# Two attention heads share a run of matmuls, rotary keys are padded to full height, and a planner's matmul durations are changed

## The chip, the core and the metric

The kernel runs on one NeuronCore of a Trainium2 chip. The metric is device time in microseconds (us) for one execution of the whole program; lower is better. The core's engines work side by side, each with its own queue in program order: TensorE (PE) multiplies matrices into PSUM, VectorE (DVE) and ScalarE (ACT) do elementwise work and reductions, GpSimd (POOL) small side work, and SyncE (SP) issues the transfers from DRAM. PE loads one operand of a matmul ahead of it; the profile shows these loads as a line of their own, PEld.

## What is computed

Four transformer layers over 256 tokens of width 1024, all in float32: a layer with block attention (MoBA) and forgetting attention (FOX), one with differential and sliding-window attention, and two blocks of latent or stick-breaking attention, cross attention to a memory and a squared-ReLU MLP. The change touches the attention of the first two layers and the latent attention (MLA) of the third. Cut to these:

```python
HEAD_DIM = 64                      # MoBA, FOX, differential maps, sliding window: 8 heads each (4 x 2 maps)
MLA_HEADS, MLA_NOPE, MLA_ROPE, MLA_V = 8, 128, 64, 128

def fox_attention(q, k, v, log_f):            # (B, H, S, 64); MoBA with one block is the same with another bias
    ...
        s = (jnp.einsum('bhqd,bhsd->bhqs', qb, k).astype(jnp.float32) * scale
             + cb[..., None] - c[:, :, None, :])
        s = jnp.where(tpos[:, None] >= kpos[None, :], s, -jnp.inf)
        p = jax.nn.softmax(s, axis=-1).astype(v.dtype)
        return jnp.einsum('bhqs,bhsd->bhqd', p, v)

def diff_attention(q, k, v, lam, slopes):     # two maps for each of 4 heads, 64 deep, values 128 wide
    ...
        p = jax.nn.softmax(s, axis=-1)
        a = (p[:, :, 0] - lam * p[:, :, 1]).astype(v.dtype)
        return jnp.einsum('bhqs,bhse->bhqe', a, v)

def swa_attention(q, k, v, sinks, slopes):    # 8 query heads, 2 key heads, window of 128
    ...

def mla_mixer(h, cos, sin, w_dkv, g_q, g_kv, w_uq, w_ukv, w_o):
    ...
    q_pe = apply_rope(q[..., MLA_NOPE:], cos, sin)
    k_pe = apply_rope(k_pe, cos, sin)
    q = jnp.concatenate([q[..., :MLA_NOPE], q_pe], axis=-1)
    k = jnp.concatenate([kv[..., :MLA_NOPE],
                         jnp.broadcast_to(k_pe, (B, S, MLA_HEADS, MLA_ROPE))], axis=-1)
    v = kv[..., MLA_NOPE:]
    o = blocked_causal_softmax_attn(q, k, v, (MLA_NOPE + MLA_ROPE) ** -0.5)
    return o.reshape(B, S, MLA_HEADS * MLA_V) @ w_o
```

## The kernel before

**Two passes.** `describe` first records every instruction of the network, with no address and no order between engines (`Plan.op`, `make`). Then `Plan.schedule` (L244) simulates the engines: it gives every instruction a duration from `make` (L472), keeps a queue for each engine by critical path and boost, lets an instruction start when what it depends on is done, and picks the engine for those that any of several may run (`either`). What comes out is a fixed order for each engine and a slot for each tile. All compute instructions are emitted from one line, L533, so the profile's rows have that line and are told apart by shape and tile. The tile names are those of the pools: `psum` the eight PSUM banks, `r` float32r tiles (the halves of split weights and activations), `k` float32 tiles; the order adds the tile's number (`psum_114`).

**Projections** are done as three float32r matmuls each (high by high, high by low, low by high half). A weight piece of 512 KB comes by DMA, ACT copies its high half, DVE subtracts the low half. These float32r matmuls are most of PE's 6829 instructions, and the planner puts them between the attention's steps.

**Attention** is in float32, where one product is two instructions on PE. Tokens are two tiles of 128, and the causal blocks are (first queries, first keys), 128 columns, and (second queries, all keys), 256 columns. The heads are 64 deep and two heads share a transposed tile: one on partitions 0 to 63, one on 64 to 127. For each head `scores` (L997) multiplies its 64 rows into a PSUM bank of its own, `soft` does the softmax on DVE and ACT, `probs_T` transposes the probabilities on PE, and `pv_feat` (L1078) multiplies values of 64 columns by them, into partitions 0 to 63 or 64 to 127 of one bank for the pair: a product with the first keys (256 columns) and one with the second (128). So a score matmul is 64 rows of the array by 128 columns (64\*128 in the profile), a value matmul 128 by 64 (128\*64), and everything else that matters 128 by 128. There are 16 pairs of score heads or maps (eight in the first layer, four differential, four sliding window) and 12 pairs of value products (eight and four; the differential values are 128 wide).

**Latent attention** (L1267) has eight heads with 128 plain dimensions and 64 rotary ones. The rotary queries of two heads share a tile by halves; the one rotary key, the same for all heads, is stored twice, in either half (`kpT`, L1319). The scores are a full-height product plus a 64-row one on the head's half, for each causal block.

The planner's durations for PE are the lines below; a float32r matmul of 256 columns counts as 109 ns.

```python
        elif mv.dtype == F32R:
            cost = N * (1 if N >= 256 else 4) / 2.4 + 2
        else:
            cost = 2 * max(2 * N / 2.4, load) + 2
```

Of the kernel before, what the change touches and what calls it, by code (L numbers as in the profile page):

```python
# [15 lines left out]
OP = mybir.AluOpType  # L16
# [4 lines left out]
# ======================================================================  # L21
# Recording: views of tiles that have no address yet
# ======================================================================
class Buf:
    """A tile to be: its slot is picked when its first instruction is scheduled."""

    def __init__(self, tag, np_, shape, dtype, name):
        self.tag, self.np_, self.dtype, self.name = tag, np_, dtype, name
        self.row = int(np.prod(shape))
        self.log = []          # (op, writes, p0, p1, mask)  # L30
        self.left = 0          # accesses not scheduled yet
        self.slot = None
        self.free_at = 0.0
        self.first = self.last = None


class Pool:
    """Slots for tiles. use[i]: the slots in use while instruction i runs, if from now on all
    instructions ran in the order of the program; as long as that fits, no deadlock is possible."""
# [114 lines left out]
# how long after the end of an instruction another engine may start  # L154
# [11 lines left out]
class Plan:  # L166
# [7 lines left out]
    # -- tiles  # L174
# [3 lines left out]
    def tag(self, name, pool, most=99, dtype=F32):  # L178
        """A kind of tile that lives in a pool, at most `most` at a time as long as others wait."""
# [12 lines left out]
    # -- instructions  # L192
    def op(self, forms, reads, writes, kind=""):
        """forms: {engine: (ns, call)}: the engines it may run on."""
        o = Op()
# [5 lines left out]
        for v, w in [(v, False) for v in reads] + [(v, True) for v in writes]:  # L201
# [13 lines left out]
            for e in b.log:  # L215
# [4 lines left out]
                # an older access that this write hides entirely need not be kept  # L220
# [11 lines left out]
    def either(self, *calls):  # L232
        """One instruction that any of several engines may run: (engine, method, args, kw) each."""
# [9 lines left out]
    # -- scheduling  # L243
    def schedule(self):  # L244
# [36 lines left out]
        def can(b):  # L281
            tg = self.tags[b.tag]
            p = tg["pool"]
            if b.first <= front:
                return bool(p.free)
            if not p.free or tg["used"] >= tg["most"]:
                return False
            return p.use[front:b.first].max() < p.bufs
# [11 lines left out]
        while n < len(ops):  # L300
# [23 lines left out]
            if e == "T":  # L324
                # the first by priority that the loading of its operand doesn't delay
# [10 lines left out]
            bad = next((b for b in news if not can(b)), None)  # L336
# [3 lines left out]
            # another engine that would be done with it sooner  # L340
# [71 lines left out]
    # -- emission  # L412
# [34 lines left out]
class _Eng:  # L447
    """Stands for an engine while the instructions are recorded."""
# [23 lines left out]
def make(plan, e, method, args, kw):  # L472
    """((cost, call), reads, writes, act tables) of one instruction."""
# [11 lines left out]
    if e == "T":  # L485
# [6 lines left out]
        elif mv.dtype == F32R:  # L492
            cost = N * (1 if N >= 256 else 4) / 2.4 + 2
        else:
            cost = 2 * max(2 * N / 2.4, load) + 2
# [57 lines left out]
# pools of tiles: elements in a partition, tiles  # L553
POOLS = {"k4": (1024, 5), "k2": (512, 33), "r2": (512, 46), "k1": (256, 18), "k128": (128, 11), "k16": (16, 64),
         "kr": (128, 3), "psum": (512, 8)}
# kinds of tiles: pool, the most at a time
# [8 lines left out]
class Net:  # L565
# [26 lines left out]
    def copy(self, out, in_):  # L592
        """A copy, on ACT or DVE."""
# [6 lines left out]
    def wpiece(self, src, f, pat, fill="", parts=1, **kw):  # L600
        """One piece of a weight matrix, f elements in each partition, as hi and lo in parts of equal size."""
# [15 lines left out]
    def wtiles(self, w, k0, nk, c0, nc_, fill=""):  # L617
        """Weight rows of the chunks k0.., columns c0..: pieces of (hi, lo, first chunk, chunks)."""
# [23 lines left out]
    def new_T(self, n=NC8):  # L642
        """(hi, lo) of a transposed activation: a list over the chunks of [128, 256] views each."""
# [9 lines left out]
    def mm3(self, ps, st, mv, first, last):  # L653
        """ps += st.T mv, both operands as (hi, lo)."""
# [5 lines left out]
    def mm_tok(self, ps, xt, wh, wl, kc, kmap, t, first, last):  # L660
        """ps[tokens of t, :] += X W, the activations stationary."""
# [8 lines left out]
    def proj_tok(self, w, xt, c0, ncol, k0=0, nk=NC8, ps=None, first=True, last=True, x0=0, cls="acc", fill=""):  # L670
        """Both token tiles of X W[:, c0:c0+ncol] in PSUM."""
# [7 lines left out]
    def mm_feat(self, ps, first_in_bank, xt, wh, wl, c, last):  # L679
        """ps[features, 256 tokens] += W.T X.T for a chunk, the weights stationary."""  # L680
# [5 lines left out]
    def proj_feat(self, w, xt, c0, ncol, nk=NC8, cls=("acc", "acc"), fill=""):  # L686
        """W[:, c0:c0+ncol].T X.T: feature blocks of 128, two to a bank."""
# [20 lines left out]
    def rows_T(self, tag, n, parts):  # L708
        """Rows of 128 from DRAM, transposed into columns [128, n]."""
# [88 lines left out]
    def squares(self, x):  # L798
        """Sums of the squares of the rows, [128, tiles]; x[t] has two halves."""
# [14 lines left out]
    def setup_late(self):  # L814
# [22 lines left out]
        nc.vector.tensor_scalar(self.lam, self.lam, LAM_INIT, None, op0=OP.subtract)  # -lambda  # L837
# [31 lines left out]
    def new_x(self):  # L869
        """The residual's transpose: banks of two chunks, [128, 2, 256] each."""  # L870
        return [self.nc.tile([128, 2, 256], "x", "x") for _ in range(4)]

    def stats_sum(self, x):
        """x: [128, k, 256] views; the sums of squares over the features, [128 tokens, tiles] in PSUM."""
# [18 lines left out]
    def stats_x(self, ss=None):  # L893
        """rstd of the residual's rows: [128, tiles]."""
# [11 lines left out]
    def gained(self, x, g0):  # L906
        """x.T times the gain, as hi and lo."""
# [11 lines left out]
    def rstd_bc(self, r):  # L919
        """rstd along the free dimension, the same in every partition: [128, 256]."""  # L920
# [10 lines left out]
    def out_proj(self, w, yt, pieces):  # L931
        """x += (Y W).T for a [*, 1024] matrix; pieces: (first chunk, chunks, half of the columns)."""
# [757 lines left out]
```

## Time and profile before

| | |
|---|---|
| three runs | 987.92, 986.16, 987.67 us; median 987.67 |
| profiled execution, span from its first to its last instruction | 990.0 us (its own time beside the span is not given) |
| PE busy | 962.9 us (97%), 6829 matmuls |
| DVE busy | 680.6 us (69%) |
| ACT busy | 571.4 us (58%) |
| POOL busy | 59.9 us (6%) |
| mean granted clock of PE | 0.994 of 2.4 GHz |

A row of the timeline gives the start of a group of like instructions that follow each other, the time from that start to the modelled end of the last, the engine, line and operation, the tiles written and read, the first one's shape (rows\*columns of the array, then the moving operand) and their number. Matmuls overlap, so the distance from one start to the next is the time that PE gives to one; the length of a row is longer than that by the part of the last one's end that lies beside the next. A row of the windows gives the busy time of each engine in a stretch, with the number of its instructions, then the granted clock and the DMA share.

### The profile page before, as it was taken

The page shows a single profiled execution, that of the slowest core. Times are in us where ns is not written, and L with a number is a line of the kernel's source. Part 1 is how long each engine was busy: PE and PEld are TensorE (multiplying, and loading weights), DVE is VectorE, ACT ScalarE, POOL GpSimd, SP SyncE. Part 2 cuts the span into 40 slices and gives each one's busy share as a digit, 9 for nine tenths or more (in the row PEclk, how much of TensorE's full clock was granted, in tenths as well). Part 3 has the DMA queues.
Part 4 walks back from the last instruction along what each step waited for, and adds up shares of the span by engine and source line. Part 5 has one row for each costly group of instructions (what it writes and reads, how often), then busy time and mean ns, then how long its engine had stood idle before and what let it go on. Part 6 is the DMA issues. An engine that isn't in the chain of part 4 may idle for free.

```text
span 990.0 us, 18191 instructions
## 1 busy us (share of the span) xinstructions
PE 962.9 (97%) x6829; PEld 874.0 (88%) x6829; DVE 680.6 (69%) x1561; ACT 571.4 (58%) x1310; POOL 59.9 (6%) x94
## 2 busy tenths in 40 slices
PE   7899999999999999999999999899999999999997
PEld 5577778888979889999999999899899999999985
DVE  7687686787987854896655456765768777556654
ACT  5675585557676675775555445644666754344443
POOL 2124000040210200000000000000000000000000
PEclk9999999999999999999999999999999999999999
DMA  7978424654413523664565456635535554555641
GB/s 193 285 191 207 113 85 150 212 149 131 145 34 90 154 94 115 211 192 141 171 204 180 149 192 203 181 128 165 166 117 168 174 170 144 179 189 176 203 154 43
DMA packets 96678, 157.13 MB, mean 159 GB/s; under 512 B 9831, under 2 KB 28493, under 8 KB 96589
## 3 DMA queue, kind: packets, MB, share of 16 engines
q1 hardware_dynamic: 96236, 154.91, 50.8%
q8 instruction: 53, 0.87, 0.4%
q0 software_dynamic: 352, 1.06, 0.3%
q14 instruction: 37, 0.30, 0.1%
HBM read 154.89 MB, written 1.06 MB: 158 GB/s over the span
## 4 chain that ended last, share of the span: by engine, by line
PE 81%; DMA 9%; DVE 4%; ACT 2%; SPq 1%; issue 1%; POOL 1%; POOLq 0%; DVEq 0%; ACTq 0%
PE psum L533 81%; DMA k<-in_w_in_ab_dram 4%; DVE r L533 2%; DMA k<-in_mlp_w_out_dram 2%; DMA k<-in_sb_w_qkv_dram 2%; ACT r L533 2%; SPq L533 1%; DVE k L533 1%; ACT k L533 1%; POOL k L533 1%; DMA k<-in_mla_w_ukv_dram 0%; DMA k<-in_mla_w_uq_dram 0%; POOLq L1686 0%; DVEq L533 0%; ACTq L533 0%
## 5 line engine op out<-in xcount | busy, mean ns | idle before, releaser
L533 PE MATMUL psum<-r,r 128*128 128x256 f32 (+2 forms) x6018 | 891.9, 305 | 9.8 <-ACT r L533 9.1
L533 PEld LDWEIGHTS psum<-r,r 128*128 128x128 f32 x6018 | 795.6, 190 | 69.1 <-ACT r L533 13.3
L533 DVE TENSOR_TENSOR r<-k,r 128x512 fp32r<-128x512 f32 (+2 forms) x669 | 407.5, 648 | 149.2 <-ACT r L533 73.1
L533 ACT ACTIVATE r<-k 128x512 fp32r<-128x512 f32 (+2 forms) x568 | 310.7, 592 | 203.7 <-PE psum L533 84.2
L533 PE MATMUL psum<-k,k 128*128 128x128 f32 (+8 forms) x771 | 149.0, 316 | 10.3 <-DMA k<-in_x_dram 4.5
L533 ACT ACTIVATE k<-psum 128x256 f32<-128x256 f32 (+4 forms) x168 | 70.5, 451 | 124.0 <-PE psum L533 120.6
L533 PEld LDWEIGHTS psum<-k,k 128*128 128x128 f32 (+3 forms) x771 | 94.9, 166 | 38.3 <-issue 12.1
L533 POOL TENSOR_TENSOR k<-k,k 128x2 f32<-128x2 f32 (+3 forms) x42 | 49.8, 1200 | 884.9 <-DVE k L533 833.5
L533 ACT ACTIVATE k<-k 128x256 f32<-128x256 f32 (+4 forms) x147 | 71.7, 507 | 19.7 <-DVE k L533 15.4
L533 ACT ACTIVATE k<-k,k 128x256 f32<-128x256 f32 (+3 forms) x152 | 64.7, 450 | 19.1 <-DVE k L533 15.9
L533 DVE CAST r<-k 128x512 fp32r<-128x512 f32 (+2 forms) x101 | 40.0, 402 | 28.9 <-PE psum L533 12.2
L533 DVE TENSOR_TENSOR k<-k 128x256 f32<-128x256 f32 (+3 forms) x40 | 13.8, 344 | 40.9 <-ACT k L533 39.6
L533 DVE TENSOR_TENSOR k<-k,k 128x512 f32<-128x512 f32 (+5 forms) x86 | 40.3, 478 | 2.3 <-ACT k L533 1.3
L533 DVE TENSOR_TENSOR k<-psum,k 128x512 f32<-128x512 f32 (+2 forms) x53 | 33.4, 635 | 11.6 <-PE psum L533 11.3
L533 ACT ACTIVATE r<-k,k 128x256 fp32r<-128x256 f32 x64 | 29.7, 500 | 16.2 <-DVE k L533 15.1
L533 DVE SCALAR_TENSOR_TENSOR r<-k,k,r 128x256 fp32r<-128x256 f32 x72 | 34.3, 494 | 2.4 <-ACT r L533 1.5
L533 DVE TENSOR_TENSOR r<-psum,r 128x256 fp32r<-128x256 f32 (+1 forms) x52 | 24.0, 480 | 16.3 <-ACT r L533 14.7
L533 ACT ACTIVATE r<-psum 128x256 fp32r<-128x256 f32 (+1 forms) x49 | 20.7, 435 | 14.1 <-PE psum L533 13.8
L533 DVE TENSOR_SCALAR k<-k,k 128x128 f32<-128x128 f32 (+7 forms) x88 | 21.6, 274 | 5.2 <-POOL k L533 4.7
L533 ACT ACTIVATE k<-psum,k 128x512 f32<-128x512 f32 (+1 forms) x18 | 11.6, 650 | 13.2 <-PE psum L533 13.2
L533 DVE CUSTOM_DVE_ANT_0 k<-psum,k 128x256 f32<-128x256 f32 (+1 forms) x48 | 15.0, 353 | 4.8 <-PE psum L533 4.5
L533 DVE CUSTOM_DVE_ANT_0 k<-psum,k,k 128x256 f32<-128x256 f32 (+1 forms) x32 | 12.1, 414 | 8.3 <-PE psum L533 8.2
(39 smaller groups left out, 165.0 us busy)
## 6 DMA issues: line engine op xcount, KB each, us to landing
k<-in_mlp_w_in_dram SPq DMA_DIRECT2D x64, 512.0 KB, 4.6
k<-in_mlp_w_out_dram SPq DMA_DIRECT2D x64, 512.0 KB, 4.5
k<-in_w_in_ab_dram SPq DMA_DIRECT2D x32, 512.0 KB, 7.0
k<-in_w_in_cd_dram SPq DMA_DIRECT2D x26, 512.0 KB, 4.6
k<-in_sb_w_qkv_dram SPq DMA_DIRECT2D x24, 512.0 KB, 4.7
k<-in_xa_w_kv_dram SPq DMA_DIRECT2D x16, 512.0 KB, 5.5
k<-in_w_out_ab_dram SPq DMA_DIRECT2D x8, 512.0 KB, 3.7
k<-in_w_out_cd_dram SPq DMA_DIRECT2D x8, 512.0 KB, 4.5
```

Source lines behind the costliest of these rows:

```text
L533: return getattr(eng, method)(*[real(a) for a in args], **{k: real(v) for k, v in kw.items()})
```

## The change

Four edits. A new `Plan.group` records several matmuls as one entry of the plan, which run one after the other. `scores` now makes both heads' products in one group (both 128-column blocks, then both 256-column blocks) into two banks, and `pv_pair` does so with the value products (both heads' first keys, then both heads' second keys), after the probabilities of both heads are transposed. The rotary key gets two tiles of 128 rows, each with one half zero, so that the rotary product is full-height and the other head's queries meet zeros. In `make`, a float32r matmul of 256 columns or more now counts as 0.4414 ns a column and 5 ns, other float32 ones as 3 ns more than before. `can` counts the other new tiles of the same entry. Comments and docstrings are gone, which shifts lines: all compute rows now stand at L552.

```diff
+    def group(self, *calls):
+        cost, load, gos, reads, writes = 190.0, None, [], [], []
+        for args, kw in calls:
+            (c, go, ld), r, w, _ = make(self, "T", "matmul", args, kw)
+            cost += 104 + 0.805 * args[2].size
+            load = ld if load is None else load
+            gos.append(go)
+            reads += r
+            writes += w
+        def go():
+            for g in gos:
+                g()
+        return self.op({"T": (cost, go, load)}, reads, writes, "group")
...
-        def can(b):
+        def can(b, before):
             tg = self.tags[b.tag]
             p = tg["pool"]
+            k = sum(self.tags[x.tag]["pool"] is p for x in before)
             if b.first <= front:
-                return bool(p.free)
-            if not p.free or tg["used"] >= tg["most"]:
+                return len(p.free) > k
+            if len(p.free) <= k or tg["used"] + sum(x.tag == b.tag for x in before) >= tg["most"]:
                 return False
-            return p.use[front:b.first].max() < p.bufs
+            return p.use[front:b.first].max() + k < p.bufs
...
         elif mv.dtype == F32R:
-            cost = N * (1 if N >= 256 else 4) / 2.4 + 2
+            cost = N * 0.4414 + 5 if N >= 256 else N * 4 / 2.4 + 5
         else:
-            cost = 2 * max(2 * N / 2.4, load) + 2
+            cost = 2 * max(2 * N / 2.4, load) + 5
...
-    def scores(self, qT, kT, rows):
-        nc = self.nc
-        s = self.ps("S")
-        nc.tensor.matmul(s[:, 0:128], qT[rows, 0:128], kT[rows, 0:128], start=True, stop=True)
-        nc.tensor.matmul(s[:, 128:384], qT[rows, 128:256], kT[rows, 0:256], start=True, stop=True)
-        return s
+    def scores(self, qT, kT):
+        res = [self.ps("S") for _ in range(2)]
+        calls = []
+        for q, k in ((slice(0, 128), slice(0, 128)), (slice(128, 256), slice(0, 256))):
+            for i, s in enumerate(res):
+                rows = slice(64 * i, 64 * i + 64)
+                o = s[:, 0:128] if q.start == 0 else s[:, 128:384]
+                calls.append(((o, qT[rows, q], kT[rows, k]), dict(start=True, stop=True)))
+        self.nc.group(*calls)
+        return res
...
+    def pv_pair(self, o, v, sls, pts):
+        calls = []
+        for k, (a, b), c in ((0, (0, 256), 0), (1, (256, 384), 128)):
+            for i, (sl, pt) in enumerate(zip(sls, pts)):
+                calls.append(((o[64 * i:64 * i + 64, c:256], v[k][:, sl], pt[:, a:b]),
+                              dict(start=k == 0, stop=k == 1, skip_group_check=True)))
+        self.nc.group(*calls)
...
             for j in range(4):
-                op = self.ps("O")[:, :256]
-                for s in range(2):
+                pts = []
+                for s, sc in enumerate(self.scores(qT[j], kT[j])):
                     h = 2 * j + s
-                    rows = slice(s * 64, (s + 1) * 64)
-                    sc = self.scores(qT[j], kT[j], rows)
...
-                    self.pv_feat(op[rows], v, slice(h * 64, (h + 1) * 64), self.probs_T(e))
+                    pts.append(self.probs_T(e))
+                op = self.ps("O")[:, :256]
+                self.pv_pair(op, v, [slice(h * 64, (h + 1) * 64) for h in (2 * j, 2 * j + 1)], pts)
...
-        kpT, = self.pairs_T([k.rearrange("p r d -> p (r d)") for k in kpd], 1)
+        p = self.ps("T")
+        for t in range(NT):
+            self.tr(p[:, t * 128:(t + 1) * 128], kpd[t].rearrange("p r d -> p (r d)"))
+        kpT = [self.t2([128, 256], "kpT") for _ in range(2)]
+        for s in range(2):
+            nc.gpsimd.memset(kpT[s][64 - 64 * s:128 - 64 * s], 0.0)
+            self.copy(kpT[s][64 * s:64 * s + 64], p[64 * s:64 * s + 64, :256])
...
-                nc.tensor.matmul(sc[:, 0:128], qpT[hh // 2][rows, 0:128], kpT[rows, 0:128], start=False, stop=True)
+                nc.tensor.matmul(sc[:, 0:128], qpT[hh // 2][:, 0:128], kpT[s][:, 0:128], start=False, stop=True)
...
-                nc.tensor.matmul(sc[:, 128:384], qpT[hh // 2][rows, 128:256], kpT[rows], start=False, stop=True)
+                nc.tensor.matmul(sc[:, 128:384], qpT[hh // 2][:, 128:256], kpT[s], start=False, stop=True)
```

The differential maps and the sliding window use `scores` in the same way, and the sliding window `pv_pair`.

How PE's order stands in the first layer's attention, before: a pair's scores are the rows that read `k_184` (keys) and `k_94` (queries), into banks 114 and 115; the other rows are float32r projections.

```order
L533 MATMUL psum_119<-r_142,r_163 128x256
L533 MATMUL psum_114<-k_184,k_94 128x128
L533 MATMUL psum_115<-k_184,k_94 128x128
L533 MATMUL psum_130<-r_150,r_131 128x512
L533 MATMUL psum_93<-r_168,r_131 128x512
L533 MATMUL psum_114<-k_184,k_94 128x256
L533 MATMUL psum_115<-k_184,k_94 128x256
L533 MATMUL psum_98<-r_123,r_110 128x256
```

The pair's 128-column and 256-column products stand apart, with two projections between.

Value products in the same layer, before: `k_194` and `k_180` are the values of the second and the first tokens, the other operand a head's transposed probabilities.

```order
L533 MATMUL psum_119<-r_131,r_113 128x256
L533 MATMUL psum_84<-k_69,k_194 64x128
L533 MATMUL psum_115<-k_217,k_194 64x128
L533 MATMUL psum_98<-r_131,r_163 128x256
L533 MATMUL psum_130<-r_168,r_142 128x512
L533 MATMUL psum_98<-r_142,r_163 128x256
L533 MATMUL psum_115<-k_76,k_180 64x256
L533 MATMUL psum_117<-k_186,k_180 64x256
```

Here two products of different banks happen to follow each other, and one head's two products lie apart.

The same stage after the change: `k_213` and `k_181` are a pair's keys and queries, `k_210` and `k_212` the values of the first and second tokens, `k_194` and `k_192` the transposed probabilities of a pair's two heads.

```order
L552 MATMUL psum_130<-r_165,r_131 128x512
L552 MATMUL psum_84<-r_165,r_131 128x512
L552 MATMUL psum_117<-k_213,k_181 128x128
L552 MATMUL psum_98<-k_213,k_181 128x128
L552 MATMUL psum_117<-k_213,k_181 128x256
L552 MATMUL psum_98<-k_213,k_181 128x256
L552 MATMUL psum_119<-r_127,r_182 128x256
L552 MATMUL psum_93<-r_135,r_147 128x256
L552 MATMUL psum_115<-k_194,k_210 64x256
L552 MATMUL psum_115<-k_192,k_210 64x256
L552 MATMUL psum_115<-k_194,k_212 64x128
L552 MATMUL psum_115<-k_192,k_212 64x128
```

All four score products of the pair stand together, and so do all four value products of another pair, in one bank.

The latent attention's scores on PE, before: `k_221` is the doubled rotary key and `k_94` the rotary queries of some heads (64-row products), the other rows are the plain part.

```order
L533 MATMUL psum_114<-k_82,k_218 128x128
L533 MATMUL psum_114<-k_221,k_94 128x128
L533 MATMUL psum_114<-k_82,k_218 128x256
L533 MATMUL psum_114<-k_221,k_94 128x256
L533 MATMUL psum_84<-k_165,k_217 128x128
L533 MATMUL psum_84<-k_221,k_94 128x128
```

And after: `k_77` is one of the two padded rotary keys and `k_69` the rotary queries, `k_210` and `k_162` keys and queries of the plain part.

```order
L552 MATMUL psum_117<-k_77,k_69 128x256
L552 MATMUL psum_93<-k_210,k_162 128x128
L552 MATMUL psum_93<-k_77,k_69 128x128
L552 MATMUL psum_93<-k_210,k_162 128x256
L552 MATMUL psum_93<-k_77,k_69 128x256
```

The products keep their places behind the plain ones; what changes is their height, which the rows don't show.

## Rows read from the trace of the kernel before

**Rows 1.** The page: span, busy times, and one group of copies on ACT.

```profile
span 990.0 us, 18191 instructions
PE 962.9 (97%) x6829; PEld 874.0 (88%) x6829; DVE 680.6 (69%) x1561; ACT 571.4 (58%) x1310; POOL 59.9 (6%) x94
...
L533 ACT ACTIVATE k<-psum 128x256 f32<-128x256 f32 (+4 forms) x168 | 70.5, 451 | 124.0 <-PE psum L533 120.6
```

**Rows 2.** The page: the chain that ended last, share of the span by engine.

```profile
PE 81%; DMA 9%; DVE 4%; ACT 2%; SPq 1%; issue 1%; POOL 1%; POOLq 0%; DVEq 0%; ACTq 0%
```

**Rows 3.** The chain in order of time: start us, us, what.

```profile
85.24 182.24 PE psum L533 x1184
...
275.14 40.24 PE psum L533 x285
...
337.79 165.72 PE psum L533 x1324
...
573.04 5.60 DMA k<-in_mlp_w_out_dram
```

**Rows 4.** Waits of PE: whole span, then 78 to 300 us (total, times, longest).

```profile
PE psum L533 <- ACT r L533: 9.1, 8, 3.7
...
PE psum L533 <- ACT k L533: 1.2, 1, 1.2
```

**Rows 5.** Windows: first layer, differential, sliding window, latent attention, a dense stretch.

```profile
78.00:158.00 80.00, 78.80 (x494) 58.24 (x494) 60.99 (x191) 53.48 (x145) 6.64 (x7) 0.98 0.49 140
214.00:230.00 16.00, 16.00 (x98) 11.92 (x97) 13.90 (x54) 10.12 (x36) 3.74 (x2) 1.00 0.33 97
268.00:296.00 28.00, 26.93 (x172) 19.10 (x172) 23.80 (x91) 21.56 (x72) 4.62 (x6) 1.00 0.20 60
337.00:373.00 36.00, 35.21 (x228) 29.14 (x229) 21.95 (x71) 25.88 (x68) 1.60 (x2) 1.00 0.38 121
440.00:460.00 20.00, 20.00 (x172) 20.00 (x171) 17.76 (x33) 11.10 (x21) 0.00 (x0) 1.00 0.50 157
```

**Rows 6.** Timeline of PE around score matmuls (64\*128).

```profile
78.85 0.49 PE L533 MATMUL psum<-k,k 64*128 64x128 f32 x2
...
95.96 0.28 PE L533 MATMUL psum<-r,r 128*128 128x256 f32 x1
96.17 0.49 PE L533 MATMUL psum<-k,k 64*128 64x128 f32 x4
96.59 1.32 PE L533 MATMUL psum<-r,r 128*128 128x256 f32 x7
97.85 0.70 PE L533 MATMUL psum<-k,k 64*128 64x256 f32 x4
...
273.27 0.93 PE L533 MATMUL psum<-k,k 64*128 64x128 f32 x8
...
277.01 0.92 PE L533 MATMUL psum<-k,k 64*128 64x128 f32 x4
```

**Rows 7.** Timeline of PE: value matmuls (128\*64).

```profile
134.82 0.65 PE L533 MATMUL psum<-k,k 128*64 128x256 f32 x4
...
139.25 0.44 PE L533 MATMUL psum<-k,k 128*64 128x128 f32 x4
...
287.66 0.86 PE L533 MATMUL psum<-k,k 128*64 128x256 f32 x6
...
293.73 1.31 PE L533 MATMUL psum<-k,k 128*64 128x256 f32 x9
...
295.52 0.43 PE L533 MATMUL psum<-k,k 128*64 128x128 f32 x2
```

**Rows 8.** Timeline of PE: a rotary product of 64 rows, and full-height float32 passes.

```profile
345.05 0.70 PE L533 MATMUL psum<-k,k 64*128 64x256 f32 x2
...
696.79 0.60 PE L533 MATMUL psum<-k,k 128*128 128x256 f32 x2
...
697.01 0.38 PE L533 MATMUL psum<-k,k 128*128 128x256 f32 x1
```

More of the change, by code (lines that the diff above doesn't have):

```diff
@@ L335, in schedule @@
             news = [b for b in o.bufs if b.slot is None]
-            bad = next((b for b in news if not can(b)), None)
+            bad = next((b for n_, b in enumerate(news) if not can(b, news[:n_])), None)
             if bad is not None:
@@ L1183, in layer_cd @@
                 sums = self.sm([128, 2, NT], "dsum")
-                for m in range(2):
-                    sc = self.scores(qT[h], kT[h], slice(m * 64, (m + 1) * 64))
+                for m, sc in enumerate(self.scores(qT[h], kT[h])):
                     e, _ = self.soft(sc, self.bias8[2 * h + 1][:, 128:256], self.bias8[2 * h + 1],
@@ L1236, in layer_cd @@
         for j in range(4):
-            op = self.ps("O")[:, :256]
-            for s in range(2):
+            pts = []
+            for s, sc in enumerate(self.scores(qT[j], kT[j // 2])):
                 h = 2 * j + s
-                rows = slice(s * 64, (s + 1) * 64)
-                sc = self.scores(qT[j], kT[h // 4], rows)
                 bw = self.t2([128, 256], "bw")
@@ L1250, in layer_cd @@
                 self.normed(e, sums)
-                self.pv_feat(op[rows], v, slice(h // 4 * 64, (h // 4 + 1) * 64), self.probs_T(e))
+                pts.append(self.probs_T(e))
+            op = self.ps("O")[:, :256]
+            self.pv_pair(op, v, [slice(j // 2 * 64, (j // 2 + 1) * 64)] * 2, pts)
             self.gated(yt, 4 + j, op, g[j], 0.5)
@@ L1373, in mla @@
                 hh = 4 * g + h
-                rows = slice(s * 64, (s + 1) * 64)
                 sc = self.ps("S")
                 nc.tensor.matmul(sc[:, 0:128], qn[h // 2][:, h % 2, 0:128], kn[h // 2][:, h % 2, 0:128], start=True, stop=False)
-                nc.tensor.matmul(sc[:, 0:128], qpT[hh // 2][rows, 0:128], kpT[rows, 0:128], start=False, stop=True)
+                nc.tensor.matmul(sc[:, 0:128], qpT[hh // 2][:, 0:128], kpT[s][:, 0:128], start=False, stop=True)
                 nc.tensor.matmul(sc[:, 128:384], qn[h // 2][:, h % 2, 128:256], kn[h // 2][:, h % 2], start=True, stop=False)
-                nc.tensor.matmul(sc[:, 128:384], qpT[hh // 2][rows, 128:256], kpT[rows], start=False, stop=True)
+                nc.tensor.matmul(sc[:, 128:384], qpT[hh // 2][:, 128:256], kpT[s], start=False, stop=True)
                 sums = self.sm([128, NT], "msum")
```

## The prediction

> **What bounds the kernel now.** I read the page first: TensorE (PE) is busy 97% of a span of 990.0 us, VectorE (DVE) 69%, ScalarE (ACT) 58% [rows 1]. The chain that ended last agrees: 81% of it is PE [rows 2]; in order of time it enters PE at 85.24 us and stays there for 182 us, again for 40 us from 275 us and for 166 us from 338 us [rows 3]. Those three pieces hold nearly all the attention code that the change touches. Third, the waits: in the whole span PE waits 9.1 us for weight halves that ACT writes, and between 78 and 300 us its longest wait is 1.2 us [rows 4]. So in the touched stages the time is the sum of what PE is given. What a matmul costs is read from the distance between starts, not from the mean of one, because they overlap: in a dense stretch 172 matmuls of 256 columns take 20 us, 0.116 each, at a granted clock of 1.00, the 2.4 GHz level [rows 5].
>
> Last, the timeline of PE around the small float32 matmuls, where the change works; each such product is two instructions there. Four (two heads, 128 columns) start at 96.17, and the next float32r matmul starts at 96.59: 0.42 inside the run. The row gives it a length of 0.49; ends are modelled, and I take 0.07 off the length of each run below [rows 6]. Before the run, the last float32r matmul holds PE from 95.96 to 96.17, 0.21 where 0.116 is usual: the entry costs 0.09. After it, seven float32r matmuls (five of 256 columns, two of 512, which I price as twice that) take from 96.59 to 97.85, 1.26, where 1.04 is usual. Of the 0.22 over, 0.09 is the entry of the next run, so leaving costs up to 0.13. I take 0.20 for both. **Every run of half-array matmuls costs 0.20 beside its content.**
>
> The content, read the same way [rows 6]: one head's 128-column block alone 0.42 (78.85), two heads' together also 0.42; two heads' 256-column blocks together 0.63; one head's two blocks in one run 0.85 (277.01); both heads' two blocks, a run of eight instructions that the old order holds once, 0.86 (273.27). The two heads stand on different halves of the array's rows and cost nothing on top of one another, and four blocks in one run cost less (0.86) than in two (1.05). Value products [rows 7]: a pair's 256 columns 0.58, its 128 columns 0.37, a single head's 128 columns 0.36 (so a single 256 is priced as the pair), six instructions 0.79.
>
> **The change part by part.**
> *Scores.* From 78.85 to 285.45 us PE runs 33 stretches of score matmuls: 18 of two heads' equal blocks (9 of 128 columns at 0.62 with the switch, 9 of 256 at 0.83: 13.1), 6 of one head's one block (4 at 0.62, 2 at 0.83: 4.1), 6 of one head's two blocks (1.05: 6.3), 2 of three blocks (1.06: 2.1), one of eight instructions (1.06). Sum 26.7 us. Afterwards 16 pairs have one stretch of eight instructions each: 16 x 1.06 = 17.0. Gain 9.7.
> *Value products.* 26 stretches, the last at 295.52: 10 of a single head (5 at 0.78, 5 at 0.56: 6.7), 13 of two (7 at 0.57, 6 at 0.78: 8.7), two of six instructions (0.99: 2.0), one of twelve, whose last nine take 1.24 (with the rest and the switch I take 1.7) [rows 7]. Sum 19.1. Afterwards there are 12 stretches of eight; the nearest row is the six at 0.79, and the two more lie beside their like, as the pairs' do: 0.80 + 0.20 = 1.00, in all 12.0. Its ends are 0.79, and 0.58 + 0.37 = 0.95 if staying in the run saves nothing. Gain 7.1, at least 5.3.
> *Rotary keys.* The eight heads of the latent layer leave full-height matmuls for half-height ones in 14 stretches: 6 at 0.62, 6 at 0.83 (one is at 345.05), two that two heads share at 0.83. Sum 10.4. With the keys padded to 128 rows there is no switch: a 256-column pass takes 0.22 (696.79 to 697.01 [rows 8]), a 128-column one half of it, so 8 x 2 x 0.33 = 5.3. Gain 5.1. The padding adds two memsets on GpSimd (busy 1.60 of 36 us there) and one more copy on ACT or DVE (25.88 and 21.95 of 36 us [rows 5]); they stand beside the weight halves and PE's own work ahead of the query projections. I set them at nothing; uncovered, the copy would cost its 0.45 [rows 1] once.
> A page of the Trainium skill speaks against the merged run: "TensorE: Matmul & The Clock Gate", Part 3, on what overlaps, says that a weight load passes a running matmul only where their row groups differ, and in a run of eight each half of the array comes round to its own rows. By that rule the run would cost 1.05, not 0.86, and 16 of them would give back 3.0 us. The trace does not agree: the run of eight at 273.27 measures 0.86.
> *Sum on PE:* 9.7 + 7.1 + 5.1 = 21.9 us, 34.3 us where 56.2 stand.
> *What comes late next.* A score run now takes two free PSUM banks at once, and a value run waits until the second head's transposed probabilities are copied; behind it on PE stands everything that is later in program order, all float32r projections too. In the piece of the new order that front.md shows for this, two float32r matmuls of 256 columns, two of 512 and a whole score run (0.23 + 0.46 + 1.06 = 1.8 us) stand between its top and the value run, against a copy of 0.45. The sliding-window stage is the tightest: DVE is busy 23.80 of 28 us [rows 5], 4.2 to spare, while PE gives up 3.1 on its scores (six runs of 1.05 and one of 1.06, to 4.2) and 2.1 on its values, 5.2 in all. So 1.0 us of the gain meets DVE. The differential stage has 2.1 us to spare (13.90 of 16) for a gain of 1.8, the first layer 19 of 80 for some 10. To the 1.0 I add one more wait of nearly the size of the longest now, 1.2 [rows 4]: 2.0 us lost, between 1.0 and 3.4 (two more).
> *Durations.* The planner's cost of a float32r matmul of 256 columns goes from 109 to 118 ns, where the trace has 116; that moves thousands of rows on all engines, and nothing in the trace prices it. From below: PE's whole wait for weight halves of ACT is 9.1 us, most of it before the touched stages, so truer due times give back some 4 at most. From above: a piece asked for late costs up to its landing, 5.60 us at 573.04 [rows 3]. I take nothing, which is what PE waits in the dense stretch of [rows 5].
> Net: 21.9 - 2.0 = 19.9 us off 990.0, a span of 970.1. Of the profiled execution only its span is known; it is 0.24% above the median of the runs, 987.67. The same 19.9 off the median gives **967.8 us**.
>
> **The rivals.**
> 1. *More than forecast.* The traced runs also hold irregular parts above my prices, the largest the wait of 1.2 [rows 4] inside a score stretch; I estimate 3.3 us for all. If merged runs shed them, late weights give back 2 and only the 1.0 at DVE is lost: 21.9 + 3.3 + 2 - 1.0 = 26.2, 961.5. For it: PE is the whole chain there. Against: a wait may come back elsewhere.
> 2. *No saving inside a run.* Runs cost 1.05 and 0.95 beside the switch: 16 x 0.19 + 12 x 0.15 = 4.8 less gained, 972.6. For it: the blocks cost that in two runs. Against: the run of eight. This is what the skill's rule above would do.
> 3. *The softmax takes over.* PE comes to a pair's value run before the second head's probabilities are there. One wait of 1.2 us at half of the 12 value runs costs 7.2, 975.0; 17 such waits over the 28 runs eat the gain whole. For it: DVE at 85% of the sliding-window stage. Against: 19 of 80 us free on DVE in the first layer, and float32r work to put between. "TensorEngine Tiling (Array Packing)" of the Trainium skill, PSUM bottleneck, warns of the same, that PSUM evacuation stays as slow when the array gets faster; no row bears it out yet.
> 4. *Slower: late weights.* With PE thought slower, splits and loads may stand later against it. Place: the first MLP, 500 to 640 us, where the chain already passes through landings [rows 3]. One exposed in each of its 8 hidden groups costs 8 x 5.6 = 45, net 1012; it decides from four exposed landings on. For it: those landings. Against: PE hardly waits for them now, and the sequence of loads on SP is nearly unchanged.
>
> **How the numbers follow.** Forecast 50%, with 963 to 973 as its own range; rival 1 14%, rival 2 12%, rival 3 16% (a quarter of it at no change), rival 4 8%. Within 0.2%, some 2 us, is about what cannot be told from no change. Faster: 50 + 14 + 12 + 12 = 88%; same 4%; slower 8%. The range runs from 959, a little below rival 1, to 981, which holds the middle of rival 3 and leaves out its tail and rival 4.
>
> **What would show it.** Between float32r matmuls 16 score stretches of about 0.86 and 12 value stretches of about 0.80; no half-height matmul after 330 us, and 16 full-height float32 products more; PE busy some 20 us less, still 96% or more of the span; PE's waits between 78 and 300 us below 5 us. Step by step wrong if a score stretch takes 1.05, if PE waits over 8 us for DVE and ACT in the attention stages, or if the chain in the first MLP shows more landings than now.

## The result, and the profile after

Four runs of the changed kernel gave a median of 996.25 us (995.0 to 1000.05), four of the kernel before on the same chip 987.13 (986.16 to 987.92): a ratio of 1.0093, 95% interval 1.0068 to 1.0118. It is slower by 9 us; 967.8 was forecast, with 959 to 981 as the range. The prediction was wrong, in its sign.

The page after, answering to [rows 1, 2]: span, busy times, and the share of the chain by engine.

```profile
span 998.3 us, 18220 instructions
PE 955.5 (96%) x6829; PEld 874.3 (88%) x6829; DVE 683.2 (68%) x1566; ACT 568.6 (57%) x1306; POOL 56.6 (6%) x96
PE 69%; DMA 14%; DVE 9%; ACT 5%; issue 2%; SPq 1%; POOL 0%; POOLq 0%; ACTq 0%; DVEq 0%
```

PE is busy for 7 us less, but stands idle for 42.8 us instead of 27.1, and its share of the chain falls from 81% to 69%. The chain of before had 267 pieces; this one leaves PE far more often. Its head line, and landings and DVE pieces from it, in order of time (start, length, what), answering to [rows 3]:

```profile
530 pieces in order of time: start us, us, what
86.12 8.46 DMA k<-cd
94.60 2.97 DVE k L552 x14
...
533.43 5.03 DMA k<-in_mlp_w_out_dram
543.89 4.67 DMA k<-in_mlp_w_out_dram
569.47 5.21 DMA k<-in_mlp_w_out_dram
...
588.74 3.62 DMA k<-in_mlp_w_out_dram
594.43 5.14 DMA k<-in_mlp_w_out_dram
```

The waits of PE over the whole span (total, times, longest), answering to [rows 4]:

```profile
PE psum L552 <- ACT r L552: 16.7, 21, 3.5
PE psum L552 <- DVE k L552: 5.2, 7, 2.0
PE psum L552 <- DMA k<-in_x_dram: 4.8, 2, 3.5
PE psum L552 <- DVE r L552: 3.8, 6, 0.8
```

Late weight halves cost 16.7 us in 21 waits, where 8 waits cost 9.1; the longest has not grown. This is no single new stall but many small ones. Between 78 and 300 us, where the first two layers' attention runs, PE's waits are 5.6 us in all, of 34.4 in the whole span, so most lie outside those stages.

Most of those matmuls came out as forecast. The timeline of PE after, around a score run and a value run, answering to [rows 6, 7]:

```profile
117.64 0.86 PE L552 MATMUL psum<-r,r 128*128 128x512 f32 x4
118.43 0.93 PE L552 MATMUL psum<-k,k 64*128 64x128 f32 x8
119.29 1.91 PE L552 MATMUL psum<-r,r 128*128 128x256 f32 x10
...
139.54 0.87 PE L552 MATMUL psum<-k,k 128*64 128x256 f32 x8
140.34 1.20 PE L552 MATMUL psum<-r,r 128*128 128x256 f32 x6
...
142.84 0.87 PE L552 MATMUL psum<-k,k 128*64 128x256 f32 x8
143.64 0.51 PE L552 MATMUL psum<-r,r 128*128 128x256 f32 x2
```

From start to next start the score run takes 0.86 and the value run 0.80. There are 16 and 12 such stretches and none of half height after 330 us; by their starts 10 of the 16 take 0.86 and 11 of the 12 take 0.80 or 0.81. Of the longer ones, one score run takes 1.59 at half clock (see the end) and one 1.45 at full clock, where the load of its third matmul waits for DVE.

So that kernels can be compared, I split each span in three: the full-height matmuls at their usual distance (0.1175 us for 256 float32r columns, 0.232 for 512, 0.216 for 256 float32 columns, and so on), the stretches of half-array matmuls (content + 0.20 each), and the rest, which holds the other waits and breaks in PE's run; a wait or lost clock inside a half-array stretch stays in its column. All numbers are worked out from the traces, in us; "planned" is the planner's duration of a float32r matmul of 256 columns in ns.

| kernel | planned | span | full height | half-array stretches (scores and rotary, values) | rest |
|---|---|---|---|---|---|
| before | 109 | 990.0 | 886.4 | 58.3 (47, 26) | 45.3 |
| after | 118 | 998.3 | 891.6 | 31.0 (16, 12) | 75.7 |
| groups_old_costs | 109 | 964.7 | 891.6 | 30.6 (15, 11) | 42.5 |
| groups_113 | 113 | 972.5 | 891.6 | 31.3 (16, 12) | 49.5 |
| groups_fast_pe | 97 | 962.1 | 891.6 | 30.2 (16, 11) | 40.3 |
| groups_slow_pe | 127 | 1003.7 | 891.6 | 30.8 (15, 11) | 81.3 |
| before_new_costs | 118 | 1023.4 | 886.4 | 70.5 (57, 37) | 66.6 |
| slow_others | 118 | 961.2 | 891.6 | 31.4 (16, 12) | 38.2 |

After against before: 22.1 us gained on PE's own work, as forecast, and 30.4 lost in the rest. Each row is one execution; those of before and after lie above their medians (for after, 1000.05 is the highest of its four).

### The profile page after: what moved, and what is told of

The parts are those of the page before. It is cut to its first block, busy times and chain, and to the rows that moved or that the text cites. A ratio compares the mean times of both kernels' runs of the same rounds, so it can differ in the third digit from the quotient of the medians.

```text
span 998.3 us, 18220 instructions
## 1 busy us (share of the span) xinstructions
PE 955.5 (96%) x6829; PEld 874.3 (88%) x6829; DVE 683.2 (68%) x1566; ACT 568.6 (57%) x1306; POOL 56.6 (6%) x96
## 3 DMA queue, kind: packets, MB, share of 16 engines
q1 hardware_dynamic: 96236, 154.91, 50.5%
## 4 chain that ended last, share of the span: by engine, by line
PE 69%; DMA 14%; DVE 9%; ACT 5%; issue 2%; SPq 1%; POOL 0%; POOLq 0%; ACTq 0%; DVEq 0%
PE psum L552 69%; DVE r L552 5%; DMA k<-in_w_in_ab_dram 5%; DVE k L552 4%; DMA k<-in_mlp_w_out_dram 3%; ACT r L552 2%; ACT k L552 2%; DMA k<-in_sb_w_qkv_dram 1%; DMA k<-in_mlp_w_in_dram 1%; DMA k<-in_mla_w_uq_dram 1%; DMA k<-cd 1%; SPq L552 1%; DMA k<-in_w_in_cd_dram 0%; DMA k<-in_mla_w_o_dram 0%; DMA k<-in_xa_w_kv_dram 0%
## 5 line engine op out<-in xcount | busy, mean ns | idle before, releaser
L552 PE MATMUL psum<-r,r 128*128 128x256 f32 (+2 forms) x6018 | 896.3, 305 | 21.0 <-ACT r L552 16.7
L552 PEld LDWEIGHTS psum<-r,r 128*128 128x128 f32 x6018 | 798.4, 189 | 80.8 <-ACT r L552 23.4
L552 DVE TENSOR_TENSOR r<-k,r 128x512 fp32r<-128x512 f32 (+2 forms) x669 | 411.5, 649 | 174.2 <-ACT r L552 84.1
L552 ACT ACTIVATE r<-k 128x512 fp32r<-128x512 f32 (+2 forms) x567 | 314.8, 594 | 207.6 <-PE psum L552 95.4
L552 PE MATMUL psum<-k,k 128*128 128x128 f32 (+8 forms) x771 | 135.8, 312 | 14.8 <-DVE k L552 5.2
L552 ACT ACTIVATE k<-psum 128x256 f32<-128x256 f32 (+4 forms) x173 | 73.6, 452 | 125.0 <-PE psum L552 121.4
L552 PEld LDWEIGHTS psum<-k,k 128*128 128x128 f32 (+4 forms) x771 | 92.4, 168 | 34.8 <-DVE k L552 11.0
L552 POOL TENSOR_TENSOR k<-k,k 128x2 f32<-128x2 f32 (+3 forms) x42 | 47.9, 1153 | 905.0 <-DVE k L552 837.7
L552 ACT ACTIVATE k<-k 128x256 f32<-128x256 f32 (+6 forms) x151 | 73.0, 505 | 20.6 <-DVE k L552 17.5
L552 ACT ACTIVATE k<-k,k 128x128 f32<-128x128 f32 (+3 forms) x147 | 62.3, 450 | 24.1 <-DVE k L552 19.7
L552 DVE CAST r<-k 128x512 fp32r<-128x512 f32 (+2 forms) x102 | 40.4, 402 | 20.5 <-PE psum L552 6.9
L552 DVE TENSOR_TENSOR k<-k,k 128x512 f32<-128x512 f32 (+5 forms) x86 | 40.0, 480 | 1.2 <-ACT k L552 0.6
L552 DVE TENSOR_TENSOR k<-psum,k 128x512 f32<-128x512 f32 (+2 forms) x53 | 33.6, 636 | 10.3 <-PE psum L552 10.0
L552 DVE TENSOR_TENSOR k<-k 128x256 f32<-128x256 f32 (+3 forms) x36 | 12.1, 337 | 39.7 <-ACT k L552 38.4
L552 DVE TENSOR_TENSOR r<-psum,r 128x256 fp32r<-128x256 f32 (+1 forms) x52 | 23.7, 481 | 19.8 <-ACT r L552 19.2
L552 DVE SCALAR_TENSOR_TENSOR r<-k,k,r 128x256 fp32r<-128x256 f32 x72 | 33.5, 489 | 2.2 <-ACT r L552 1.7
L552 ACT ACTIVATE r<-k,k 128x256 fp32r<-128x256 f32 x61 | 28.1, 498 | 11.5 <-DVE k L552 11.0
L552 ACT ACTIVATE r<-psum 128x256 fp32r<-128x256 f32 (+1 forms) x46 | 19.4, 439 | 24.4 <-PE psum L552 21.7
L552 DVE TENSOR_SCALAR k<-k,k 128x128 f32<-128x128 f32 (+7 forms) x93 | 23.3, 278 | 3.8 <-POOL k L552 2.8
L552 ACT ACTIVATE k<-psum,k 128x512 f32<-128x512 f32 (+1 forms) x16 | 10.6, 662 | 9.1 <-PE psum L552 8.5
L552 DVE CUSTOM_DVE_ANT_0 k<-psum,k 128x256 f32<-128x256 f32 (+1 forms) x48 | 14.5, 351 | 1.3 <-PE psum L552 1.3
L552 ACT ACTIVATION_READ_ACCUMULATOR k<-k,k 128x1 f32 x80 | 15.2, 189 | 0.0
```

The lines of the kernel that those rows point to most:

```text
L552: return getattr(eng, method)(*[real(a) for a in args], **{k: real(v) for k, v in kw.items()})
```

## Experiments

Each ratio is against the kernel before on the same chip, with its 95% interval; the chips differ from one group of runs to the next.

**Which part costs.** The first kernel is the changed one with the two lines of durations put back; the second is the kernel before with those two lines alone changed.

```diff
-            cost = N * 0.4414 + 5 if N >= 256 else N * 4 / 2.4 + 5
+            cost = N * (1 if N >= 256 else 4) / 2.4 + 2
...
-            cost = 2 * max(2 * N / 2.4, load) + 5
+            cost = 2 * max(2 * N / 2.4, load) + 2
```

> The changed kernel with the planner's old matmul durations (109 ns for a float32r matmul of 256 columns); the merged runs and the padded keys stay. Theory A (durations: once the planner counts PE at its true speed, it puts matmuls just where their operands come due by the plan, and on the chip loads and splits come later, so PE waits): the old cushion returns, and the 22 us saved on PE show: 965 to 972 us. Theory B (runs: a value run waits for both heads' softmax, a score run for two banks): stays slow, 988 to 996. Theory C (chance: any new order of this planner moves the waits by 1% either way): anywhere from 965 to 1000, with waits at places that have nothing to do with A or B.

967.05 us, 0.9793 (0.9767 to 0.9819).

> The kernel before with only the new matmul durations in the planner; no merged runs, no padded keys. A: slower by about what was lost, some 31 us of new waits: 1005 to 1018 us, with waits for ACT and DVE weight halves all over the span. B: no change, 984 to 990. C: anywhere from 977 to 1000.

1023.26 us, 1.0357 (1.0338 to 1.0377), above the 1005 to 1018 expected. The kernel before has 987.84 on this chip. With the durations put back, the change gives 20.8 us off the median; the durations by themselves cost 29 us in the grouped kernel (996.25 against 967.05) and 35 in the kernel before. By the table a third of the 33.4 us between the spans of these last two is no wait: the new durations also split more pairs (57 and 37 half-array stretches for 47 and 26), 12.2 us. The page and PE's waits of the first, to be held against those of after:

```profile
PE 940.1 (97%) x6829; PEld 869.1 (90%) x6829; DVE 678.8 (70%) x1565; ACT 573.1 (59%) x1311; POOL 57.0 (6%) x96
PE 78%; DMA 11%; DVE 5%; ACT 3%; issue 1%; SPq 1%; POOL 0%; POOLq 0%; DVEq 0%; ACTq 0%
...
PE psum L552 <- ACT r L552: 8.0, 11, 2.9
PE psum L552 <- DVE k L552: 3.7, 3, 2.3
```

And the waits of the second, with old matmuls and new durations:

```profile
PE psum L533 <- ACT r L533: 14.7, 15, 3.9
PE psum L533 <- DVE k L533: 7.4, 5, 2.5
```

The wait for ACT's weight halves goes with the durations, not with the runs: 9.1 and 8.0 with the old ones, 14.7 and 16.7 with the new. Where it is lost is seen in the windows of the two grouped kernels (busy time and number of instructions of each engine). First after:

```profile
78.00:300.00 222.00, 216.11 (x1497) 186.00 (x1496) 178.49 (x523) 141.30 (x368) 29.31 (x30) 0.98 0.44 130
300.00:500.00 200.00, 192.61 (x1518) 185.09 (x1517) 140.51 (x329) 119.22 (x278) 6.56 (x8) 1.00 0.47 145
500.00:640.00 140.00, 134.61 (x1111) 132.17 (x1110) 75.75 (x134) 74.09 (x156) 0.00 (x0) 1.00 0.56 181
```

And with the old durations:

```profile
78.00:300.00 222.00, 219.72 (x1575) 193.49 (x1574) 184.87 (x533) 151.30 (x383) 28.59 (x28) 1.00 0.47 138
300.00:500.00 200.00, 199.05 (x1620) 195.24 (x1619) 140.45 (x326) 128.51 (x297) 7.34 (x8) 1.00 0.50 163
500.00:640.00 140.00, 138.80 (x1166) 137.70 (x1165) 86.89 (x156) 75.42 (x157) 0.87 (x1) 1.00 0.56 185
```

PE's idle time is larger in each (5.9, 7.4, 5.4 against 2.3, 1.0, 1.2) and its matmuls are 78, 102 and 55 fewer; the third stretch is the first MLP, with no changed matmul in it. Of the 33.6 us between the two spans 18.2 are idle time on the page. The rest counts as busy: ends are modelled, and a lone 256-column matmul has 0.28 [rows 6] where the next may start after 0.116, so breaks under 0.16 hide in its length. By the distances between the starts of full-height matmuls, some 23 us more lie in distances that show idle time and some 8 in ones that are too long and show none. Up to 4.9 us of it is lost clock (see the end).

**Each other part alone**, in the kernel before with its old durations: the rotary keys padded; the score runs; the value runs. The edits are those of the diff above, one at a time.

> The kernel before with only the rotary keys padded to full height. A and B alike: PE gives up 14 stretches of half-height matmuls for 16 full-height products, 5 us less: 981 to 984 us. C: anywhere from 977 to 997, since the order changes too.

984.74 us, 0.9951 (0.9931 to 0.9971): 3.1 off by the medians, 4.8 by the ratio, 5.1 by the prediction. In its trace the half-array stretches take 48.0 us for 58.3 and the padded products 5.2 more, 5.1 off as well.

> The kernel before, with its old durations, and only the score products of two heads in one run. By the sum of the prediction PE gives up 9.7 us: 977 us (974 to 981) if the waits stay as they are. Chance theory: 970 to 995.

988.33 us, 1.0016 (1.0003 to 1.0028).

> The kernel before, with its old durations, and only the value products of two heads in one run. By the sum PE gives up 7.1 us: 980 us (977 to 984). If the wait for the second head's probabilities costs what the forecast's third rival says, 987 or more. Chance theory: 972 to 997.

993.74 us, 1.0067 (1.0045 to 1.009). The last two gain nothing alone, though together with the padding they gain 20 us under the old durations. By the traces, with score runs alone the score stretches of the first two layers take 20.4 instead of 28.9 us, but the value stretches 22.5 instead of 19.1. There are 26 of these as before, but three take 1.45, 1.45 and 2.54, against 0.80 for both stretches of six in the kernel before: no two products in them start together, and the last holds a wait of 1.03. With value runs alone these take 11.7 instead of 19.1, but the score stretches 30.5, and the rest grows from 45.3 to 50.5 us. Part of both is lost clock:

```profile
260.00:280.00 20.00, 17.95 (x121) 15.18 (x119) 19.22 (x59) 15.70 (x46) 7.29 (x9) 0.89 0.30 92
280.00:300.00 20.00, 20.00 (x144) 17.03 (x143) 12.81 (x48) 11.85 (x40) 0.00 (x0) 0.85 0.08 25
```

These are the windows of value runs alone; the granted clock is 0.89 and 0.85 where the sliding-window stage of before has 1.00 [rows 5], 5.2 us of clock in 40. Some 2.9 of it lie in three score stretches (2.93, 1.58 and 1.58, where like ones take 1.50 and 0.85). So the parts' ratios can't be added: each carries the accidents of its own order.

**Is it PE's duration as such?** Theory A of the expectations: what counts is PE's planned speed against that of the others. In the plan that the code of the kernel before makes, the durations add up to some 520 us on ACT where the trace has 571 busy, and to 639 on DVE where it has 681. A 512 KB load is planned to land after about 3.5 us, where the page's medians are 3.7 to 7.0 (last figure of a row):

```profile
k<-in_mlp_w_in_dram SPq DMA_DIRECT2D x64, 512.0 KB, 4.6
...
k<-in_w_in_ab_dram SPq DMA_DIRECT2D x32, 512.0 KB, 7.0
...
k<-in_w_out_ab_dram SPq DMA_DIRECT2D x8, 512.0 KB, 3.7
```

So before, ACT, DVE and PE were planned some 6 to 9% short and most loads by more, and the change sets right PE alone. Rivals: the true duration is bad by itself, or any new order is a draw. First PE planned still shorter:

```diff
-            cost = N * 0.4414 + 5 if N >= 256 else N * 4 / 2.4 + 5
+            cost = N * 0.36 + 5 if N >= 256 else N * 4 / 2.4 + 5
```

> The changed kernel with PE counted still faster in the plan (0.36 ns a column and 5 ns: 97 ns for 256 columns, where the trace has 116). A: the cushion is larger than before the change, waits on PE fall to those of the old durations or below: 960 to 970 us. B: 988 to 996. C: no order between this and the run with the old durations.

962.93 us, 0.9743 (0.9721 to 0.9765). The waits:

```profile
PE psum L552 <- DVE k L552: 4.2, 5, 2.3
PE psum L552 <- ACT r L552: 3.9, 3, 3.4
```

PE waits 3.9 us for weight halves, a quarter of what it waits in after. With 0.3, 0.476 and 0.4225 ns a column for 0.36 (82, 127 and 113 ns for 256 columns):

> The changed kernel with PE counted faster still in the plan: 0.30 ns a column and 5 ns, 82 ns for 256 columns. Theory A (cushion) alone: nothing left to win once PE hardly waits, 958 to 965 us. Rival: a plan this far from the chip picks a poor order, 966 to 985.

972.31 us, 0.9852 (0.9817 to 0.9886).

> The changed kernel with PE counted slower than it is: 0.476 ns a column and 5 ns, 127 ns for 256 columns against 116 in the trace. Theory A (cushion: the faster PE is planned against the other engines, the less it waits): slower than with 118 ns, 1000 to 1020 us. Rival (118 ns happened to give a bad order): about as the other plans, 965 to 985.

1006.03 us, 1.0194 (1.0162 to 1.0227).

> The changed kernel with a float32r matmul of 256 columns counted as 113 ns, half way between the old duration (109, run at 967 us) and the new (118, 996). Theory A as a slope (waits grow steadily with the planned duration): 976 to 986 us. A as a step (the plan turns bad only where PE is planned slower than the others): 964 to 972 or 990 to 998. Chance: either, with the extra time in one place.

973.9 us, 0.9874 (0.9859 to 0.9889). In order of the duration, 82, 97, 109, 113, 118, 127 ns: 972, 963, 967, 974, 996, 1006 us. It has a best place near 97, where the plan has PE faster than it is, and falls off on both sides, most steeply from 113 to 118: neither a straight slope nor one step (113 came out between the ranges of the two). The same shorter duration for float32r in the kernel before:

> The kernel before with only the planner's float32r duration changed, to 0.36 ns a column and 5 ns (97 ns for 256 columns). Theory A: PE's waits fall by some 4 us as they did between 109 and 97 ns with the merged runs: 980 to 986 us. Chance theory: 975 to 1000.

996.74 us, 1.0107 (1.0072 to 1.0141): slower by 9 us, where theory A said 980 to 986. Theory A misses here. The rest falls from 45.3 to 43.0, as it has it, but the half-array stretches grow from 58.3 to 63.7 (45 and 33 of them). That is 3.1 us between the two traced executions; the other 6 us between the medians are not explained. What theory A says of shorter durations is thus shown for the grouped kernel alone.

**The others set right.** PE stays at 118 ns; ACT and DVE get the trace's durations, or the loads, or both:

```diff
+    if e == "A" and method != "dma_start":
+        cost *= 1.1
+    if e == "V":
+        cost *= 1.065
...
-                o.start, o.end = t, st + d + 1500
+                o.start, o.end = t, st + d + 2700
```

> The changed kernel with its new matmul durations, and the planner's durations for ScalarE raised by 10% and for VectorE by 6.5%, so that their sums come to the busy times of the trace; loads are left as planned. Theory A1 (what hurts is that PE alone was set to its true speed while ACT and DVE stayed planned too short): back to 966 to 976 us. Theory A2 (what hurts are loads that the plan lands after 3.5 us and the chip after 4.4 to 5.2): little gained, 986 to 996. Theory D (a true duration for PE is bad by itself, whatever the others have, as only a PE planned too fast leaves a cushion for everything the plan doesn't hold): 988 to 998.

974.54 us, 0.9872 (0.9835 to 0.9908).

> The changed kernel with its new matmul durations, and every load landing 1.2 us later in the plan (4.7 us after its issue for a 512 KB piece, near the trace's median); ACT and DVE as planned. A1: little gained, 986 to 996 us. A2: 966 to 976. D: 988 to 998.

972.53 us, 0.9849 (0.9821 to 0.9877).

> The changed kernel with its new matmul durations, and both ACT, DVE and the loads set near the trace in the plan. A1 and A2 alike: 963 to 974 us, as good as the old durations with the merged runs (967). D: 985 to 998.

970.0 us, 0.9821 (0.9791 to 0.9851). The rest is 48.7, 45.3 and 38.7 us, against 75.7; the half-array stretches are 30.5, 33.9 and 36.2, against 31.0, as a few hold waits. In the last of the three, PE's waits for weight halves are down from 16.7:

```profile
PE psum L556 <- ACT r L556: 6.1, 5, 3.1
```

The duration of 118 ns is therefore not bad by itself; it is bad beside others that are planned too short. Either correction alone brings back 22 or 24 of the 29 us; why either is enough is open. With more than the truth, factors of 1.2 and 1.16 and the same loads:

> The changed kernel with its new matmul durations and the planner's durations for ACT raised by 20%, for DVE by 16%, loads landing 1.2 us later: all others planned slower than they are. Theory A (what counts is how PE is planned against the rest): at least as good as with true durations (970) and near the 963 that came of planning PE too fast: 960 to 972. Theory E (only true durations for all give a good plan): 975 to 990.

962.63 us, 0.9765 (0.9745 to 0.9785), the same as with PE planned at 97 ns. The ratios fit theory A: 118 ns beside ACT at 1.2 corresponds to 98 beside ACT at 1, and beside ACT at 1.1 to 107. With ACT at 1, 97 and 109 ns gave 963 and 967, against 962.63 and 970.0 here (974.54 where the loads were left as planned). PE's 89% of the chain answers to [rows 2]:

```profile
by line: PE psum L556 89.4%; DMA k<-in_w_in_ab_dram 2.8%; SPq L556 1.4%; DMA k<-in_xa_w_kv_dram 1.3%; DVE r L556 1.1%; ACT k L556 0.7%; DMA k<-in_mlp_w_out_dram 0.6%; DMA k<-in_mla_w_uq_dram 0.6%; issue 0.5%; DVE k L556 0.5%; ACT r L556 0.5
166 pieces in order of time: start us, us, what
```

**A fourth load buffer** (`k4` 6, `raw` at most 4, `r2` 44), with 118 and with 97 ns:

> The changed kernel with its new durations, with a fourth buffer for weight pieces on their way in, taken from the split halves (44 tiles for 46). If PE waits because a load's landing is too late in the ring of three buffers (theory A2), a piece more in flight covers it: 966 to 978 us. If the planned order itself is late at splits and in the attention (A1): 985 to 997.

992.69 us, 1.006 (1.0037 to 1.0084).

> The kernel with merged runs and PE planned at 97 ns (963 us), with the same fourth buffer for weight pieces. PE's waits there are 14 us in all, some 4 of them for late weight halves: 957 to 963 us if the buffer removes these; 963 to 970 if the two split tiles fewer cost more.

966.51 us, 0.9802 (0.9787 to 0.9817). By the medians it wins 3.6 us under the new durations, which is not clear of the noise (the intervals of the ratios overlap), and loses 3.6 under the short ones, so too few load buffers are not the main cause. Two split tiles were given up for it, which muddies the size.

That any new order is a mere draw doesn't fit the twelve grouped plans taken together: the three with PE at 118 or 127 ns beside the old durations of the others take 993 to 1006 us, the nine others 963 to 975.

## Why the prediction was wrong

- *Durations: wrong, and this alone turned the sign.* The step reads "I take nothing". The runs put 29 us there (967.05 to 996.25). The reason given, that PE waits for nothing in the dense stretch, says nothing of the other stages or of a new order. I had asked whether PE's new number was nearer to the trace's 116, and it is; I hadn't asked how the planner's numbers for ACT, DVE and the loads stand to the trace. Its bound from above was one exposed landing, 5.6, for thousands of moved rows.
- *Rival 4 had the right sign, and late weights as it said, but the wrong place and price.* It set one exposed landing of 5.6 in each hidden group of the first MLP, 45 us. Landings do stand in the chain there, but PE's waits for weight halves are short (16.7 us in 21 waits over the whole span, 8.0 with the old durations), and the loss is spread over all stages.
- *Scores, values, rotary keys: right.* 21.9 us were worked out, 34.3 left of 56.2. The traces give 22.1 off after and 22.5 off with the old durations: 0.86 for most score runs, 0.80 for most value runs, and 5.1 for the padding in its own trace.
- *What comes late next: about right.* With old durations the median falls by 20.8 (17.9 to 23.0 by the ratio's interval), so some 1.1 of 21.9 are lost, where 2.0 were taken; the interval holds both. The traces would put this loss below nothing (rest 42.5 against 45.3), but the profiled execution of before was longer than its median run, so this term is not settled.
- *Rival 2 falls.* The rule of the Trainium skill that I set beside it ("TensorE: Matmul & The Clock Gate", Part 3, that a weight load passes a running matmul only where the row groups differ) would make a score run 1.05. At full clock 10 of the 16 runs measure 0.86.
- *Signs named beforehand.* PE was to be busy some 20 us less (7), to wait under 5 us between 78 and 300 us (5.6), and the chain was to show no more landings in the first MLP than before (between 500 and 640 us 8 of MLP weights for 5, of all weights 9 for 8): these say wrong. The runs' lengths and counts say right.

What stays open: by which steps of the plan a longer duration of PE makes splits late, and at which place each begins, why the loss is steepest between 113 and 118 ns, and how much of any one ratio within 1% is the draw of an order rather than its cause.

## What to carry to other kernels

A static plan is steered by the ratios between its durations. Setting one engine's number to the trace while the others stayed too short cost 29 us here. Correcting the others as well brought 26 of them back (970.0). Keeping the bound engine a little too fast did better in the grouped kernel (962.93), but lost 9 us in the ungrouped one, so such a choice has to be measured. And price a table of numbers that moves every row by the whole wait it can open, not by the nearest single stall.

## What the runs showed of the hardware

A run of short waits can cost twice, once as idle time and once as clock. After, PE waits 1.99, 0.79 and 0.72 us between 94 and 101 us, and the granted clock falls to 0.50, the 1.2 GHz level, as the windows show (PE, PEld, DVE, ACT, POOL, then clock, DMA share, GB/s):

```profile
94.00:98.00 4.00, 1.49 (x8) 0.89 (x6) 3.40 (x16) 2.79 (x6) 0.00 (x0) 0.94 0.57 225
98.00:102.00 4.00, 3.01 (x11) 2.39 (x13) 3.97 (x10) 2.08 (x6) 0.00 (x0) 0.50 0.00 0
102.00:106.00 4.00, 4.00 (x18) 3.05 (x19) 2.74 (x9) 1.26 (x3) 0.00 (x0) 0.50 0.67 131
106.00:110.00 4.00, 4.00 (x27) 3.88 (x27) 2.02 (x4) 2.38 (x6) 0.00 (x0) 0.78 0.84 240
```

The score run in it, from the timeline:

```profile
101.79 1.65 PE L552 MATMUL psum<-k,k 64*128 64x128 f32 x8
103.38 0.79 PE L552 MATMUL psum<-r,r 128*128 128x256 f32 x2
```

It takes 1.59 instead of 0.86. PE is busy throughout from 102 us and still at half rate for four more; from 98 to 110 us up to 4.9 us of clock are given up (4 x 0.5, 4 x 0.5, 4 x 0.22). The kernel with value runs alone shows the same: PE is busy for 2.69 of the 4 us from 272 us, and the next 8 us, with PE busy throughout, have a granted clock of 0.50.
